# Hybrid decoder trunk on one core: the output projection in two halves of 512 columns, halved constants folded into copies, the first loads in one queue, and a new table of ranks

## The chip, the cores and the metric

The kernel runs on 1 core of one Trainium2 chip. The metric is the device time of one execution in microseconds (us); lower is better. An engine is called here by its short name: PE (TensorE; PEld is its weight load), DVE (VectorE), ACT (ScalarE), POOL (GpSimd), SP (SyncE, which issues most DMAs).

## The reference, cut to what matters

Two layers over x of 512 tokens by 1024 channels, float32. In each layer one input projection feeds four mixers A to D of 256 channels each; their gated outputs are joined and go through one output projection, which is added to the residual. A final RMSNorm ends the trunk.

```python
h = rmsnorm(x, norm_w)
p = split_cols(h @ w_in)            # 1024 x 3380 per layer
o_a = dsa_mixer(...)                # indexer, top 128 of the keys, attention
o_b = nsa_mixer(...)                # compressed, selected and window attention
y = conv3(p['c_c'] * p['c_x'], conv_w);  o_c = p['c_b'] * y
o_d = einsum(causal_pool_mean(d_u) - d_u, pool_w) * pool_scale
mixed = concat([silu(gate_m) * o_m for m in 'abcd'])
x = x + mixed @ w_out               # 1024 x 1024 per layer
```

## The kernel before, in words

**Tiling.** Tokens stand in four tiles of 128 (index `i`), channels in eight blocks of 128 (index `k`). Every product with a large weight is done as three matmuls of split float32 values: high part times high part, high times low, low times high. `lin_tok` (line 603) makes a tile of tokens by `n` columns with 8 x 3 matmuls of `n` columns each into one PSUM bank (tag "mm", two banks); `lin_ch` (line 616) makes 128 channels by 512 tokens.

**Weights.** `load_w` (line 568) brings a group of up to 384 columns in four parts of two channel blocks. A part is: a DMA into a staging tile `st` (four places), a copy to the high part `wh` (ACT; for the very first group, `start=True`, DVE), and a subtraction for the low part `wl` (POOL, one for each channel block; for the first group the second one is DVE's). `wh` and `wl` have six places each of 2 x 384 columns. Two groups of layer 0 stage in the places of `mT` instead (`ws`).

**The start.** `load_x` brings the x tiles by SP's queue, the first weight part goes by ACT's queue (two DMAs, line 582), the other three by SP's. `norm_tile` (line 746) squares each half of an x tile (first half on ACT with a POOL step behind it, second half on DVE: `mean_sq`, line 719), takes the power on POOL, scales on DVE (`xn`), transposes on PE and splits into `hT` (ACT and DVE). 40 transposes of `warm` (line 655) fill PE where nothing else is ready.

**Constants.** `late_constants` (line 703) fills the masks on POOL, issues 14 small DMAs on SP (`cw`, `pw`, `psc`) and then makes two halved copies with POOL: `cwh = 0.5 * cw` and `psh = 0.5 * psc`, which `conv` and `conv_gate_pool` (lines 1196, 1214) read on DVE much later.

**The output projection** of layer `l` (from line 1300): three groups of columns, 256 + 384 + 384 in layer 0 and 384 + 384 + 256 in layer 1; in each group the four token tiles (`out_tile`, line 1309) run over the channel blocks in the order `KORD` = 4, 5, 6, 7 (mixers C, D), 0, 1 (A), 2, 3 (B). DVE adds the residual, ACT squares for the next norm, POOL sums. In layer 0 the next layer's first weight group is loaded and its norm runs beside the last group; in layer 1 `store` (line 1323) scales and writes the result.

**What sets the order.** The whole kernel is recorded (`Tape.record`) as operations in numbered stages (every call of a function marked `staged`). `schedule` (line 396) then writes a fixed order for each engine: at each step the operation that can start soonest by a table of modelled costs (`cost`, line 318), and among those that start within 1 ns the one of the lowest rank; `RANK` (line 195) holds one rank for each stage. An engine runs its list strictly in that order and waits on semaphores. DMAs on SP are in the list too: one that needs no place that is still held is issued as soon as SP is free.

Of the kernel before, what the change touches and what calls it, by code (L numbers as in the profile page):

```python
# [18 lines left out]
P = 128  # L19
# [147 lines left out]
class Weights:  # L167


    def __init__(self, part):  # L170
        self.part, self.parts = part, {}

    def __getitem__(self, h):
        if h not in self.parts:
            self.parts[h] = self.part(h)
        return self.parts[h]
# [7 lines left out]
class Engine:  # L184
# [43 lines left out]
class Tape:  # L228
# [89 lines left out]
    def cost(self, op):  # L318
# [9 lines left out]
        if op.name == "dma_start":  # L328
# [4 lines left out]
            if op.eng == "ACT" and sum(o.eng == "ACT" for o in self.ops) == 2:  # L333
                op.occ += 1280
# [61 lines left out]
    def schedule(self):  # L396
# [49 lines left out]
        while len(order) < len(ops):  # L446
# [23 lines left out]
            if op.name == "dma_start":  # L470
                landing = max(s + 2000, landing) + op.seen - 2000
                op.seen = landing - s
# [914 lines left out]
```

## Time and profile before

| what | us |
|---|---|
| median of 3 runs | 540.31 (540.21 to 543.2) |
| the profiled execution's own time | 540.52 |
| its span, first to last instruction | 538.8 |
| PE busy | 523.2 (97%) |
| DVE, ACT, POOL busy | 410.4, 301.5, 318.0 |

Rows of the profile name an operation as out<-in by the program's tile names; in the timeline the columns are start, time from the first start to the last end of a merged run of like operations, engine, operation, shapes, count, and in brackets the idle time of the engine before it with what ended it. Almost every instruction carries line 523, the one call that plays the list, so tiles tell the rows apart. PE's matmuls overlap: the length of one is more than the distance from one to the next. The granted clock is a share of full speed: 1.00 is 2.4 GHz, 0.5 is 1.2 GHz.

### The profile page before, as it was taken

The numbers are of one execution on the slowest core, as the hardware profiler recorded it, in microseconds if no ns is written. First come the engines' busy times: TensorE is split into PE (matmuls) and PEld (weight loads), VectorE is DVE, ScalarE is ACT, GpSimd is POOL, SyncE is SP. The second block draws the span as 40 slices with busy tenths as digits, with TensorE's granted clock in tenths as the row PEclk, the third lists the DMA queues.
The fourth block names the chain that finished last, engine by engine and source line by source line (L and its number), as shares of the span: only waits on it lengthen the run. The fifth ranks groups of instructions, "written<-read, shape, count | busy, mean of one in ns | idle before, by whom it ended". The sixth has DMA issues, their size and how long they took to land.

```text
span 538.8 us, 9722 instructions
## 1 busy us (share of the span) xinstructions
PE 523.2 (97%) x3091; PEld 459.5 (85%) x3091; DVE 410.4 (76%) x1151; ACT 301.5 (56%) x735; POOL 318.0 (59%) x492
## 2 busy tenths in 40 slices
PE   7979999999999999999999999999999999999995
PEld 6979987778888887899999989778888878789995
DVE  4936799999988868751384689999999987887424
ACT  3447655555648576653245775644366846765422
POOL 5737654475368584836674765447564558693632
PEclk9989999999999999999999999999999999999998
DMA  8960221544133111236751433236413220212204
GB/s 256 260 168 10 77 71 39 128 117 120 31 87 82 37 53 46 54 101 183 207 156 50 119 90 81 49 102 162 110 40 78 61 58 31 88 47 73 78 1 157
DMA packets 74163, 50.63 MB, mean 94 GB/s; under 512 B 23288, under 2 KB 68480, under 8 KB 74112
## 3 DMA queue, kind: packets, MB, share of 16 engines
q1 hardware_dynamic: 73408, 49.38, 33.8%
q10 hardware_dynamic: 704, 0.64, 0.4%
q8 instruction: 24, 0.39, 0.3%
q14 instruction: 27, 0.22, 0.1%
HBM read 45.81 MB, written 4.19 MB: 93 GB/s over the span
## 4 chain that ended last, share of the span: by engine, by line
PE 78%; DVE 11%; DMA 4%; issue 3%; POOL 1%; ACT 1%; SPq 0%; ACTq 0%; POOLq 0%; DVEq 0%
PE mm L523 57%; PE tr L523 10%; PE s L523 6%; PE pv L523 6%; DVE acc L523 5%; DMA st<-in_w_in_dram 3%; DVE m L523 2%; POOL wl L523 1%; DVE qb L523 1%; DMA x<-in_x_dram 1%; DVE qiT L523 1%; SPq L523 0%; ACT qiT L523 0%; ACT wh L523 0%; DMA cw<-in_conv_w_dram 0%
## 5 line engine op out<-in xcount | busy, mean ns | idle before, releaser
L523 POOL TENSOR_TENSOR wl<-st,wh 128x384 fp32r<-128x384 f32 (+4 forms) x188 | 177.9, 974 | 79.2 <-ACT wh L523 63.2
L523 PE MATMUL mm<-hT,wh 128*128 128x512 f32 x544 | 180.4, 403 | 0.7 <-DVE vA L523 0.4
L523 PEld LDWEIGHTS mm<-hT,wh 128*128 128x128 f32 x544 | 99.4, 188 | 19.6 <-DVE vA L523 1.3
L523 PE MATMUL mm<-wh,hT 128*128 128x360 f32 (+3 forms) x480 | 108.6, 310 | 0.5 <-ACT junk L523 0.5
L523 PE MATMUL mm<-hT,wl 128*128 128x512 f32 x272 | 106.5, 400 | 0.0
L523 PE MATMUL mm<-wh,mT 128*128 128x384 f32 (+1 forms) x384 | 90.2, 321 | 0.4 <-DVE x L523 0.4
L523 ACT ACTIVATE wh<-st 128x768 fp32r<-128x768 f32 (+4 forms) x92 | 70.8, 777 | 30.2 <-PE mm L523 17.8
L523 PEld LDWEIGHTS mm<-wh,hT 128*128 128x128 f32 x480 | 80.9, 192 | 1.4 <-ACT junk L523 0.8
L523 PE MATMUL mm<-wl,hT 128*128 128x360 f32 (+3 forms) x240 | 73.2, 311 | 3.1 <-POOL wl L523 3.1
L523 PEld LDWEIGHTS mm<-wh,mT 128*128 128x128 f32 x384 | 66.2, 189 | 2.3 <-DVE x L523 1.0
L523 ACT ACTIVATE pb<-pb,mn 128x128 f32<-128x128 f32 (+3 forms) x96 | 53.3, 557 | 17.9 <-DVE mn L523 17.4
L523 PE MATMUL mm<-wl,mT 128*128 128x384 f32 (+1 forms) x192 | 59.6, 322 | 0.0
L523 PEld LDWEIGHTS mm<-hT,wl 128*128 128x128 f32 x272 | 51.1, 188 | 9.5 <-POOL wl L523 0.8
L523 ACT ACTIVATE ph<-tr 128x512 fp32r<-128x512 f32 x68 | 38.1, 595 | 29.0 <-PE tr L523 22.4
L523 DVE MAX8 m<-acc 128x8 f32<-128x512 f32 (+2 forms) x96 | 51.4, 550 | 0.5
L523 DVE MATCH_REPLACE8 acc<-m,acc 128x512 f32<-128x512 f32 (+2 forms) x96 | 51.7, 541 | 0.0
L523 PEld LDWEIGHTS mm<-wl,hT 128*128 128x128 f32 x240 | 45.8, 192 | 3.9 <-POOL wl L523 3.5
L523 DVE TENSOR_TENSOR pl<-tr,ph 128x512 fp32r<-128x512 f32 x60 | 39.9, 685 | 9.4 <-ACT ph L523 8.4
L523 POOL TENSOR_SCALAR pb<-pb,rs,gt 128x512 f32<-128x512 f32 (+2 forms) x48 | 33.7, 715 | 20.7 <-DVE rs L523 6.6
L523 PE MATMUL tr<-ident,pb 128*128 128x128 f32 x240 | 44.2, 274 | 0.0
L523 DVE TENSOR_TENSOR x<-mm,x 128x256 f32<-128x256 f32 (+2 forms) x32 | 12.7, 420 | 38.3 <-PE mm L523 38.3
L523 PEld LDWEIGHTS tr<-ident,pb 128*128 128x128 f32 x240 | 30.9, 140 | 9.6 <-POOL pb L523 2.1
(162 smaller groups left out, 900.3 us busy)
## 6 DMA issues: line engine op xcount, KB each, us to landing
st<-in_w_in_dram SPq DMA_DIRECT2D x104, 128.0 KB, 2.6
st<-in_w_in_dram SPq DMA_DIRECT2D x28, 256.0 KB, 3.2
st<-in_w_out_dram SPq DMA_DIRECT2D x16, 384.0 KB, 3.4
x<-in_x_dram SPq DMA_DIRECT2D x16, 256.0 KB, 4.2
st<-in_w_in_dram SPq DMA_DIRECT2D x7, 320.0 KB, 3.9
st<-in_w_out_dram SPq DMA_DIRECT2D x8, 256.0 KB, 2.7
x1d<-x SPq DMA_DIRECT2D x8, 256.0 KB, 3.3
x<-x1d SPq DMA_DIRECT2D x8, 256.0 KB, 2.8
```

What stands on the lines that cost most here:

```text
L523: getattr(self.engines[op.eng].real, op.name)(*[real(a) for a in op.args], **{k: real(v) for k, v in op.kw.items()})
```

## The change

- **Output projection.** Two halves of 512 columns (`load_half`, one channel block per part) in both layers; only the last token tile's last half in layer 1 is done as two products of 256 columns. A part is now one DMA of 128 x 512, one ACT copy and one POOL subtraction. The split weights get single places: for half 0 six channel blocks in the places of `wh` and `wl` and two (2, 3) in places of the tag `cd` (tiles of `conv` and `conv_gate_pool`); for half 1 blocks 4 and 5 in those of `sga` and `sgb` (gates of mixers A and B), 6 in `kTA0`, `kTA1`, 7 in `vA`, `kiT`, and 0 to 3 in `wh`, `wl`.
- **Constants.** `cwh` and `psh` are gone: the factor 0.5 stands as `scale=0.5` in two ACT copies that were there already. The 14 DMAs and the clearing of `pw` move to a stage of their own, `channel_constants`, recorded after `compressed`; its rank is 105 (`late_constants`, which had 127, has 72).
- **First loads.** All on SP's queue. The ranks of the first stages put them in the order x tile 0, weight part 0, part 1, x tile 1, part 2, x tile 2, part 3, x tile 3 (11, 17, 20, 21, 22, 23, 24, 25); before it was x tiles 0, 1, 2, then parts 1, 2, then x tile 3, part 3. The copies to `wh` of the first group go from DVE to ACT.
- **First norms.** `early`: for token tile 0 as before; for tiles 1 to 3 both halves are squared on ACT, with a POOL step behind each.
- **Stores.** In layer 1 the second half of every token tile is stored by ACT's queue (before: of the last tile alone).
- **Ranks and cost table.** A new `RANK`, 540 instead of 480 ns for a DMA's issue and longer landings early in the kernel, in the model that orders the work.

```diff
@@ -167,13 +167,15 @@
-    def __init__(self, part):
-        self.part, self.parts = part, {}
-
-    def __getitem__(self, h):
+    def __init__(self, part, per):
+        self.part, self.per, self.parts = part, per, {}
+    def __getitem__(self, k):
+        h = k // self.per
         if h not in self.parts:
             self.parts[h] = self.part(h)
-        return self.parts[h]
+        return self.parts[h][k % self.per]
@@ -193,34 +195,33 @@
 RANK = [
-    1, 0, 577, 3, 5, 0, 576, 28, 38, 2, 6, 4, 29, 34, 27, 42, 0, 30, 39, 22, 40, 0, 45, 43, 44, 12, 0, 32, 0,
...
+    1, 11, 571, 54, 2, 0, 0, 17, 20, 21, 22, 23, 24, 25, 6, 18, 0, 29, 26, 32, 42, 0, 33, 37, 36, 38, 0, 8, 0,
...
 ]
@@ -328,9 +329,9 @@
             rows = n * (out.shape[0] if out is not None else P) * 4 // run
-            op.dur = op.occ = 480
+            op.dur = op.occ = 540
             op.seen = 2000 + rows * (0.56 + run / 437.0)
-            if op.eng == "ACT" and sum(o.eng == "ACT" for o in self.ops) == 2:
+            if op.eng == "ACT" and not any(o.eng == "ACT" for o in self.ops):
                 op.occ += 1280
@@ -468,7 +469,8 @@
             if op.name == "dma_start":
-                landing = max(s + 2000, landing) + op.seen - 2000
+                landing = max(s + 2000, landing)
+                landing += (op.seen - 2000) * (1.4 if landing < 8000 else 1.15 if landing < 15000 else 1.0)
                 op.seen = landing - s
@@ -579,7 +581,7 @@
             for c0, c in segs:
-                (S if start and h == 0 else SP).dma_start(
+                SP.dma_start(
                     st[:, :, o : o + c],
@@ -587,15 +589,26 @@
             wl = wp.tile([P, 2, 384], F32R, name=nm("wl"), tag="wl", bufs=6)
-            if start:
-                V.tensor_copy(wh[:, :, :n], st[:, :, :n])
-            else:
-                S.activation(wh[:, :, :n], st[:, :, :n], AF.Copy)
+            S.activation(wh[:, :, :n], st[:, :, :n], AF.Copy)
             for k in range(2):
                 lo(V if start and k else G, wl[:, k, :n], st[:, k, :n], wh[:, k, :n])
-            return wh, wl
-
-        return Weights(part)
+            return [(wh[:, k, :], wl[:, k, :]) for k in range(2)]
+        return Weights(part, 2)
+    def load_half(src, b, homes):
+        @tape.staged
+        def part(k):
+            st = wp.tile([P, T], F32, name=nm("st"), tag="st", bufs=4)
+            SP.dma_start(st, src[k * P : (k + 1) * P, half(b)])
+            hi, lw = homes(k)
+            S.activation(hi, st, AF.Copy)
+            lo(G, lw, st, hi)
+            return [(hi, lw)]
+        return Weights(part, 1)
@@ -605,8 +618,7 @@
         for k in order:
-            wh, wl = w[k // 2]
-            rh, rl = wh[:, k % 2, c0 : c0 + n], wl[:, k % 2, c0 : c0 + n]
+            rh, rl = (v[:, c0 : c0 + n] for v in w[k])
             st, sp = k == order[0], k == order[-1]
@@ -617,8 +629,7 @@
         for k in range(KC):
-            wh, wl = w[k // 2]
-            lh, ll = wh[:, k % 2, c0 : c0 + P], wl[:, k % 2, c0 : c0 + P]
+            lh, ll = (v[:, c0 : c0 + P] for v in w[k])
             PE.matmul(ps, lh, act[0][:, k, :], start=k == 0, stop=False)
@@ -680,8 +691,6 @@
     pw = const.tile([P, DEPTH, 2, P], F32, name="pw")
-    cwh = const.tile([P, DEPTH, 3, 2], F32, name="cwh")
-    psh = const.tile([P, DEPTH, 2], F32, name="psh")
@@ -706,6 +715,9 @@
                             channel_multiplier=1)
+    @tape.staged
+    def channel_constants():
         G.memset(pw, 0.0)
@@ -713,8 +725,6 @@
             SP.dma_start(psc[:, l, :], pool_scale[l].rearrange("(j p) -> p j", p=P))
-        G.tensor_scalar(cwh, cw, 0.5, 0.0, op0=OP.mult, op1=OP.add)
-        G.tensor_scalar(psh, psc, 0.5, 0.0, op0=OP.mult, op1=OP.add)
@@ -731,11 +741,11 @@
-    def rms(xt, g, ms=None):
+    def rms(xt, g, ms=None, early=False):
             for b in range(2):
-                ms = mean_sq(xt[b], ms, b == 1)
+                ms = mean_sq(xt[b], ms, b == 1 and early)
         G.tensor_tensor(ms, ms, mhalf, OP.pow)
@@ -743,8 +753,8 @@
     @tape.staged
-    def norm_tile(i, xt, g, hT, ms=None):
-        xn = rms(xt, g, ms)
+    def norm_tile(i, xt, g, hT, ms=None, early=False):
+        xn = rms(xt, g, ms, early)
         ts = slice(i * P, (i + 1) * P)
@@ -1196,16 +1206,16 @@
             b = cd()
-            S.activation(b, pb, AF.Copy)
+            S.activation(b, pb, AF.Copy, scale=0.5)
             p = lin_ch(hT, w, P)
             y = cd()
-            V.tensor_scalar(y, u, cwh[:, l, 2, j : j + 1], None, op0=OP.mult)
+            V.tensor_scalar(y, u, cw[:, l, 2, j : j + 1], None, op0=OP.mult)
             for s in (1, 2):
-                V.scalar_tensor_tensor(y[:, s:], u[:, : T - s], cwh[:, l, 2 - s, j : j + 1], y[:, s:], op0=OP.mult,
+                V.scalar_tensor_tensor(y[:, s:], u[:, : T - s], cw[:, l, 2 - s, j : j + 1], y[:, s:], op0=OP.mult,
                                        op1=OP.add)
@@ -1220,7 +1230,7 @@
             u, a, b = cd(), cd(), cd()
-            S.activation(u, ps, AF.Copy)
+            S.activation(u, ps, AF.Copy, scale=0.5)
@@ -1243,7 +1253,7 @@
             PE.matmul(pm, pw[:, l, j, :], a, start=True, stop=True)
-            V.scalar_tensor_tensor(u, pm, psh[:, l, j : j + 1], b, op0=OP.mult, op1=OP.mult)
+            V.scalar_tensor_tensor(u, pm, psc[:, l, j : j + 1], b, op0=OP.mult, op1=OP.mult)
             mixed(6 + j, u)
@@ -1275,6 +1285,8 @@
         compressed(cmp_in)
+        if l == 0:
+            channel_constants()
         w = load_w(win, [(B_GATE, 256)])
@@ -1301,23 +1313,21 @@
         g = load_g(SP, norm_w[l + 1 : l + 2, :] if l + 1 < DEPTH else final_norm_w[None, :])
-        c0 = 0
         ms = [None] * NT
         y = [norm_out() if fin else None for _ in range(NT)]
-        @tape.staged
-        def out_tile(i, w, c0, n):
-            ps = bank("mm", 2)
-            lin_tok(ps, mT, i, w, 0, n, KORD)
-            for b in range(2):
-                a, e = max(c0, b * T), min(c0 + n, (b + 1) * T)
-                if a < e:
-                    r = slice(a - b * T, e - b * T)
-                    xo = xn[i][b][:, r]
-                    V.tensor_add(xo, ps[:, a - c0 : e - c0], xo)
-                    ms[i] = mean_sq(xo, ms[i], e == DM)
-                    if fin:
-                        V.tensor_mul(y[i][b][:, r], xo, g[b][:, r])
+        @tape.staged
+        def out_tile(i, w, b):
+            n = T // 2 if fin and b and i == NT - 1 else T
+            for c in range(0, T, n):
+                ps = bank("mm", 2)
+                lin_tok(ps, mT, i, w, c, n, KORD)
+                xo = xn[i][b][:, c : c + n]
+                V.tensor_add(xo, ps[:, :n], xo)
+                ms[i] = mean_sq(xo, ms[i], b == 1 and c + n == T)
+                if fin:
+                    V.tensor_mul(y[i][b][:, c : c + n], xo, g[b][:, c : c + n])
@@ -1329,21 +1339,40 @@
             S.activation(y[i][1], y[i][1], AF.Copy, scale=ms[i])
-            (S if i == NT - 1 else SP).dma_start(out[i * P : (i + 1) * P, half(1)], y[i][1])
-
-        for n in (384, 384, 256) if fin else (256, 384, 384):
-            w = load_w(w_out[l], [(c0, n)])
-            last = c0 + n == DM
-            if last and not fin:
+            S.dma_start(out[i * P : (i + 1) * P, half(1)], y[i][1])
+        def home(pool, tag, bufs=1):
+            return pool.tile([P, T], F32R, name=nm("w"), tag=tag, bufs=bufs)
+        def homes_0(k):
+            if k in KORD[6:]:
+                return home(wk, "cd", 4), home(wk, "cd", 4)
+            return home(wp, "wh", 6), home(wp, "wl", 6)
+        spare = {}
+        def homes_1(k):
+            j = KORD.index(k)
+            if j < 2:
+                if not spare:
+                    spare.update((s, res.tile([P, 2, T], F32R, name=nm("w"), tag=s)) for s in ("sga", "sgb"))
+                return spare["sga"][:, j, :], spare["sgb"][:, j, :]
+            if j < 4:
+                return [home(res, t) for t in (("kTA0", "kTA1"), ("vA", "kiT"))[j - 2]]
+            return home(wp, "wh", 6), home(wp, "wl", 6)
+        for b, homes in enumerate((homes_0, homes_1)):
+            w = load_half(w_out[l], b, homes)
+            if b and not fin:
                 w_next = first_group(l + 1)
             for i in range(NT):
-                out_tile(i, w, c0, n)
-                if last:
+                out_tile(i, w, b)
+                if b:
                     store(i)
                         norm_tile(i - 1, xn[i - 1], g, hT_next, ms[i - 1])
-            c0 += n
         if not fin:
@@ -1351,7 +1380,7 @@
     def first_norm(i):
-        norm_tile(i, xt0[i], g_first, hT0)
+        norm_tile(i, xt0[i], g_first, hT0, early=i == 0)
```

## Rows read from the trace of the kernel before

**Rows 1.** Page: busy time and share by engine; granted PE clock in 40 slices.

```profile
PE 523.2 (97%) x3091; PEld 459.5 (85%) x3091; DVE 410.4 (76%) x1151; ACT 301.5 (56%) x735; POOL 318.0 (59%) x492
...
PEclk9989999999999999999999999999999999999998
```

**Rows 2.** Stretches: length; busy PE, PEld, DVE, ACT, POOL (instructions); clock, DMA share, GB/s.

```profile
12.00:16.40 4.40, 3.54 (x24) 2.82 (x22) 4.40 (x10) 1.78 (x5) 2.38 (x5) 1.00 1.01 324
20.00:33.00 13.00, 13.00 (x90) 12.85 (x88) 8.60 (x28) 7.76 (x25) 5.55 (x12) 1.00 0.78 163
34.20:37.40 3.20, 0.11 (x1) 0.00 (x0) 0.60 (x2) 0.57 (x2) 1.10 (x4) 1.00 0.55 151
37.40:41.00 3.60, 3.56 (x16) 3.46 (x16) 0.00 (x0) 0.00 (x0) 3.60 (x8) 0.53 0.80 241
```

**Rows 3.** Waits of PE, whole span: total us, times, longest.

```profile
PE mm L523 <- POOL wl L523: 3.1, 1, 3.1
```

**Rows 4.** Timeline, 29 to 38 us: the constants' stage and the weights behind it.

```profile
29.20 1.15 ACT L523 ACTIVATE wh<-ws 128x512 fp32r<-128x512 f32 x2
...
34.62 0.20 POOL L523 TENSOR_SCALAR cwh<-cw 128x12 f32<-128x12 f32 x1 [7.92 <-DMA cw<-in_conv_w_dram]
...
36.50 0.20 POOL L523 TENSOR_SCALAR psh<-psc 128x4 f32<-128x4 f32 x1 [1.68 <-DMA psc<-in_pool_scale_dram]
36.66 2.79 POOL L523 TENSOR_TENSOR wl<-ws,wh 128x256 fp32r<-128x256 f32 x4
...
37.44 0.49 PE L523 MATMUL mm<-wl,hT 128*128 128x256 f32 x1 [3.13 <-POOL wl L523]
```

**Rows 5.** Timeline, 0 to 12 us: first loads, first norm, first matmul.

```profile
0.79 2.91 SPq L523 DMA_DIRECT2D x<-in_x_dram  x6
...
1.42 0.92 ACTq L523 DMA_DIRECT2D st<-in_w_in_dram  x2
...
3.75 4.96 SPq L523 DMA_DIRECT2D st<-in_w_in_dram  x4
...
6.09 0.56 POOL L523 TENSOR_TENSOR ss<-ss,mhalf 128x1 f32<-128x1 f32 x1 [0.88 <-DVE ss L523]
...
8.37 0.54 DVE L523 CAST wh<-st 128x720 fp32r<-128x720 f32 x1 [2.36 <-DMA st<-in_w_in_dram]
...
9.39 1.40 DVE L523 SCALAR_TENSOR_TENSOR xn<-x,ss,s 128x512 f32<-128x512 f32 x2
...
11.80 0.41 PE L523 MATMUL mm<-wh,hT 128*128 128x360 f32 x1
```

**Rows 6.** Groups by shape, PE, in 144:153, 246:255 and 526:532 us: busy us, mean ns.

```profile
L523 PE MATMUL mm<-hT,wh 128*128 128x512 f32 x27 | 8.2, 389 | 0.0
L523 PE MATMUL mm<-hT,wl 128*128 128x512 f32 x14 | 5.3, 389 | 0.0
...
L523 PE MATMUL mm<-wh,mT 128*128 128x384 f32 x35 | 8.8, 334 | 0.0
L523 PE MATMUL mm<-wl,mT 128*128 128x384 f32 x19 | 5.9, 334 | 0.0
...
L523 PE MATMUL mm<-wh,mT 128*128 128x256 f32 x36 | 6.5, 283 | 0.0
L523 PE MATMUL mm<-wl,mT 128*128 128x256 f32 x17 | 4.8, 283 | 0.0
```

**Rows 7.** Groups by shape, POOL, whole span: busy us, mean ns, idle before, releasers.

```profile
L523 POOL TENSOR_TENSOR wl<-st,wh 128x384 fp32r<-128x384 f32 x112 | 115.0, 1054 | 59.6 <-ACT wh L523 46.8 <-PE mm L523 8.9 <-DMA st<-in_w_in_dram 3.4
...
L523 POOL TENSOR_TENSOR wl<-st,wh 128x256 fp32r<-128x256 f32 x40 | 29.6, 768 | 11.1 <-ACT wh L523 10.9
```

**Rows 8.** Chain that ended last, from 499 us: start us, us, what.

```profile
499.07 30.93 PE mm L523 x199
```

**Rows 9.** Timeline, 500 to 503 us, layer 1: the last use of mixer A's gate.

```profile
500.62 0.43 DVE L523 SCALAR_TENSOR_TENSOR om<-om,sg 128x256 f32<-128x256 f32 x1
...
501.31 2.17 POOL L523 TENSOR_TENSOR wl<-st,wh 128x384 fp32r<-128x384 f32 x2 [6.97 <-ACT wh L523]
```

53 rows, old and new, of the table RANK are left out of this document.

## Prediction

> **What bounds the kernel now.** I read the page first. PE is busy 97% of the span and no other engine more than 76% [rows 1]: PE's list of work is the bound nearly everywhere, and time is won by shortening it or by closing the few places where PE stands still or runs slow. The line of granted clock shows where: an 8 in the third slice (27 to 40 us) and one at the end [rows 1]. The waits of PE name one large one, 3.1 us for POOL's low parts of weights [rows 3]. The timeline around it tells why: PE waits until 37.44 us for `wl`; POOL could have made it from about 30 us, since ACT had the high parts ready at 29.20 + 1.15 = 30.35, but POOL stood 7.92 us at `cwh`, for the DMA of the convolution's constants, and 1.68 us more at `psh` [rows 4]. Nobody needs these constants yet. Behind the pause PE is granted 0.53 of its clock from 37.4 to 41 us, that is mostly 1.2 instead of 2.4 GHz [rows 2]. The stretches ahead show the start: between 12 and 16.4 us DVE is busy all of the 4.40 us, the DMA engines are full (324 GB/s), PE has 3.54 of 4.40, part of it filler; from 20 to 33 us PE is full [rows 2].
>
> The sum is made against the profiled execution's own 540.5 us (span 538.8 and 1.7 around it), which is 0.2 above the median of 540.31. About 1% (5.4 us) is what a measurement of this kernel can tell from no change.
>
> **Constants (likely -4.8 us).** The two POOL operations go, and with them both waits. POOL's next four `wl` took 2.79 us [rows 4]; begun at 30.4 they end near 33.2, before PE asks for the first of them at about 34.3 (37.44 - 3.13). So the 3.13 us of standing go. The clock: 37.4 to 41 us holds 16 matmuls of 256 columns in 3.56 us [rows 2]; at the full-clock distance found below (0.118 us) they take 1.9, so 1.7 us more go with the pause, if the low clock follows from it, as its place right behind it says. 3.1 + 1.7 = 4.8. Bounds: 2.4, if half of it comes back as a wait for the next thing POOL is late with, and 4.8; a loss is excluded, because an operation and its wait leave POOL's list and DVE reads the constants only in `conv`. The 14 small DMAs stay on SP's queue. Their rank puts them later, but having nothing to wait for they will still go out in the first gaps, ahead of weights for later groups as now; cost nothing, since PE is full from 20 to 33 us with them in the queue [rows 2]. If that cover goes, it is a late weight part and belongs to rival 1.
>
> **Start (likely -2.5 us).** The power for x tile 0 is ready at 6.09 + 0.56 = 6.65 us, but DVE scales the tile only at 9.39: in its list the first CAST stands ahead, waiting 2.36 us for weight part 0 until 8.37, then a `wl` [rows 5]. The first matmul starts at 11.80. Part 0 is that late because ACT's two issues at 1.42 share the DMA engines with six x loads of SP [rows 5]; in the new order it is second in line, and the cast is ACT's. So DVE can scale 9.39 - 6.65 = 2.7 us earlier, and the transposes and the first matmul follow. DVE, full from 12 to 16.4 us [rows 2], also loses four casts and three squaring passes; ACT, which takes them, is busy 1.78 of those 4.40 us and has room. What follows is fed in the order in which it is used. Upper bound 2.7 + (4.40 - 3.54) = 3.6 us, if PE also becomes full in that stretch; lower bound -0.9 (a loss), the 0.92 us that ACT's queue spent on issuing and SP's now spends [rows 5], if the rest is paced by DMA throughput. I take 2.5, near the gap that one can read off DVE's list. It carries through to the end, because PE is the bound behind it.
>
> On the issue: the Trainium skill, "DMA: Bandwidth & Descriptors" (section "Issuing engines are not separate DMA queues"), says that DMAs of all issuing engines run on the same 16 DMA engines and that a second issuing engine saves only issue time. That speaks against the change, for it gives up that saving. The trace agrees in part: SP's six x issues take 2.91 us, the next four 4.96 us with the DMA engines full [rows 5]: they wait for throughput, not for issue. By the rule alone the term would be 2.5 - 0.9 = 1.6; I leave it at 2.5.
>
> **Output projection (likely -1.0 us).** The distance of matmuls in full stretches is (stretch + one length) / count of those that touch it [rows 6]: 512 columns (9.0 + 0.389) / 41 = 0.229 us; 384: (9.0 + 0.334) / 54 = 0.173; 256: (6.0 + 0.283) / 53 = 0.1185. A block of 1024 columns costs 2 x 0.173 + 0.1185 = 0.4645 before, 2 x 0.229 = 0.458 after: 6.5 ns less. There are 2 layers x 4 tiles x 24 = 192 of them: 1.25 us. The last tile's split gives back 24 x (0.237 - 0.229) = 0.2. So 1.0. The fixed part of the matmuls saved (192 fewer, 24 more by the split) is the whole gain there. Weights: POOL's `wl` takes 1.054 us at 384 and 0.768 at 256 columns [rows 7], so 1.34 at 512 (estimate on the line through both), 8 x 1.34 = 10.7 a half against 22.0 us of PE work (96 x 0.229): hidden, with little room where the halves meet (rival 2). The tail behind the last matmul keeps its 256 columns and its steps; storing more by ACT's queue costs nothing, since those are early tiles.
>
> On the distance: the Trainium skill, "TensorE: Matmul & The Clock Gate" (section "Back-to-back issue gap"), gives N / 2.4 + 2.5 ns for an isolated matmul at full clock, a smaller fixed part than the rows have. By it a block saves 2.5 ns and the term would be 0.5 us; the rows decide.
>
> **Order of the rest (0, bounds -3 and +3).** All ranks change. PE idles 538.8 - 523.2 = 15.6 us in all [rows 1]; 3.1 is counted, and most of the rest is start and tail. What remains, and the slack hidden in busy time, I bound by 3 us both ways, as an estimate. I take 0.
>
> **Sum.** 540.5 - 4.8 - 2.5 - 1.0 = 532.2 us.
>
> **Rivals.**
> 1. *POOL stays the supplier that is late* (537.1 us). PE comes earlier to the second early group, whose low parts are also POOL's, so half of the constants' gain returns as a shorter pause and the start's gain ends in the same wait: 540.5 - 2.4 - 1.0. For it: PE's only large wait is for `wl` [rows 3]. Against: POOL gets 9.6 us of waiting back [rows 4] and is busy 5.55 of 13 us before [rows 2].
> 2. *The halves meet badly* (541.8 us, slower than before). Blocks 4 and 5 of half 1 take the places of mixer A's gate, last read at 500.62 + 0.43 = 501.05 in layer 1 [rows 9]. 199 of 288 matmuls are still ahead at 499.07 [rows 8], so 89 x 0.173 = 15.4 us of projection are done there; of the 22.0 us of half 0 then 6.6 are left, to 505.7. POOL makes blocks 4, 5 from about 501.7 (one ACT copy) to 504.4 and 0 to 3 to 509.7; PE, after 12 matmuls of half 1, wants block 0 at 508.4 and block 3 at 510.5. That holds with 0.8 us to spare, if 6 and 7 are made before in POOL's idle 6.97 us [rows 9]. If they are not, or the copies stand in ACT's list behind something late, PE pauses. A pause like the one at 34 us cost 4.8 with its low clock; one per layer makes 532.2 + 9.6. It decides once POOL has about 0.8 us more to do. Against: the second PSUM bank gives 2.75 us of other work.
> 3. *The new order also wins in the middle* (529.2 us): the bound of -3. For it: the landings in the model that orders the work come later, so loads are planned earlier. Against: little of PE's idle time lies there.
>
> **Chances.** Forecast 0.52, rival 1 0.20, rival 2 0.14, rival 3 0.14. The forecast's own range is 529.5 to 535. The whole range, 527 to 540, takes in rivals 1 and 3 with their bounds and leaves out most of rival 2. Faster by over 1% (below 534.9): rival 3 and nearly all of the forecast, 0.64. Within 1%: rival 1, most of rival 2 and the forecast's rest, 0.30. Slower by over 1% (above 545.7): rival 2 with the start's gain gone too, 0.06.
>
> **What would show it.** Right: no POOL wait for `cw` or `psc`; PE has no wait near 34 us and full clock from the start to the tail; the first `hT` matmul near 9.3 us; the projection's 512-column matmuls 0.229 us apart without a PE wait for `wl` at the change of halves; PE's idle time down from 15.6 us by 3 or more. Wrong: a second slice of low clock, a PE wait for `wl` between 30 and 60 us (rival 1) or in the projection (rival 2), a first matmul at 11 us or later.

## The result, and the profile after

The kernel after takes 538.66 us (median of 20 executions, 531.98 to 540.23) beside 541.29 for the kernel before (20 executions): ratio 0.9926, 95% interval 0.9905 to 0.9948. By this ratio, which goes by the mean of the executions, the gain is some 4.0 us; the two medians differ by 2.6 us. Forecast were 8.3 us less. The single executions tell more than the median: four of the 20 took 531.98 to 533.68, the other sixteen 536.8 to 540.2. The mean granted clock was 0.998 or 0.999 in each of the four and 0.990 to 0.996 in the sixteen. The profiled one (538.69, span 536.8) belongs to the sixteen.

The page of the profile after: busy times, then the two lines that answer to [rows 1].

```profile
PE 521.5 (97%) x2923; PEld 442.2 (82%) x2923; DVE 418.3 (78%) x1119; ACT 303.6 (57%) x723; POOL 307.6 (57%) x462
...
PE   8999999999999999999999999999969999999995
...
PEclk9999999999999999999999999999979999999998
```

The 8 that the granted clock had in its third slice is gone. A 7 has come where nothing was: slice 30, 389 to 403 us, in layer 1. PE's own line has a 6 in the same slice. The waits of PE, which answer to [rows 3], name the new pause:

```profile
PE tr L525 <- DVE pl L525: 4.5, 1, 4.5
PE tr L525 <- POOL ident L525: 1.7, 1, 1.7
PE mm L525 <- ACT w L525: 1.1, 1, 1.1
```

The 3.1 us for POOL's `wl` are gone, 4.5 us for DVE's `pl` are there. The windows, the first four over the stretches of [rows 2], the last two around the new pause (columns: us, then busy and count of PE, PEld, DVE, ACT, POOL; granted clock, DMA share, GB/s):

```profile
12.00:16.40 4.40, 4.24 (x31) 3.79 (x29) 3.29 (x6) 3.64 (x9) 3.66 (x7) 1.00 1.07 361
20.00:33.00 13.00, 13.00 (x92) 12.79 (x91) 7.29 (x26) 7.57 (x23) 7.75 (x17) 1.00 0.47 92
34.20:37.40 3.20, 3.20 (x29) 3.20 (x28) 2.57 (x9) 1.66 (x7) 2.97 (x7) 1.00 0.91 319
37.40:41.00 3.60, 3.60 (x33) 3.60 (x32) 2.40 (x10) 3.16 (x8) 0.87 (x2) 1.00 0.43 158
393.90:398.80 4.90, 0.44 (x3) 0.05 (x3) 4.90 (x4) 0.00 (x0) 3.33 (x4) 0.75 0.55 147
396.40:403.20 6.80, 4.43 (x15) 3.77 (x16) 5.65 (x16) 2.42 (x9) 0.83 (x1) 0.50 0.47 115
```

The pause at 34 to 37 us and the low clock behind it have gone as forecast: PE is full there at 1.00. The last two rows show the same pair again, only later and larger: PE stands for most of 4.9 us, and from 396.4 to 403.2 us it is granted 0.50, that is 1.2 instead of 2.4 GHz. The timeline from 389 to 400 us tells what DVE was doing:

```profile
391.41 5.82 POOL L525 TENSOR_TENSOR wl<-st,wh 128x384 fp32r<-128x384 f32 x6
...
391.61 5.91 DVE L525 TENSOR_SCALAR cd<-cd,cw 128x512 f32<-128x512 f32 x1
...
393.91 0.40 PE L525 MATMUL pv<-ph,vB 128*128 128x512 f32 x1
...
397.44 0.68 DVE L525 MAX8 m<-acc 128x8 f32<-128x512 f32 x1
398.04 1.26 DVE L525 TENSOR_TENSOR pl<-tr,ph 128x512 fp32r<-128x512 f32 x2
...
398.77 0.48 PE L525 MATMUL tr<-ident,pb 128*128 128x128 f32 x1 [4.46 <-DVE pl L525]
```

One DVE operation, the convolution's first product `cd = cd * cw`, takes 5.91 us. It begins 0.20 us after the start of the first of six `wl` subtractions that POOL runs back to back, and ends 0.29 us after the end of the sixth. Behind it in DVE's list stand a `MAX8` and the `pl` for which PE waits. The operations of the tile `cw`, after and then before, show how unusual that is (durations min/median/max in ns, then first and last start):

```profile
L525 DVE TENSOR_SCALAR cd<-cd,cw x4: 476/960/5910, 138.3 to 430.8; 128x512 f32<-128x512 f32 x4
```

```profile
L523 DVE TENSOR_SCALAR cd<-cd,cwh x4: 582/757/1306, 148.4 to 430.9; 128x512 f32<-128x512 f32 x4
```

The chain of work that ended last, followed back between 375 and 410 us, runs through it:

```profile
391.69 5.83 DVE cd L525
397.52 0.60 DVE m L525
398.12 0.60 DVE pl L525
398.77 0.48 PE tr L525
```

To see where the time went over the whole span, take for each trace the time from the span's start less what PE's matmuls begun by then would take at the distances of [rows 6] (about 8.5 ns each, plus 0.434 ns a column; the 40 transposes of `warm` count as nothing). What is left is the time that PE has lost so far, idle, slow or on filler. It is an estimate, worked out from the start of every other matmul in the trace:

| lost in us between | before | after | difference |
|---|---|---|---|
| start and 33 us | 14.0 | 11.9 | -2.1 |
| 33 and 60 (constants) | 7.1 | 2.2 | -5.0 |
| 60 and 240 (layer 0) | 12.8 | 11.1 | -1.7 |
| 240 and 300 (projection of layer 0, change of layers) | 3.0 | 5.2 | +2.2 |
| 300 and 385 | 6.3 | 5.5 | -0.8 |
| 385 and 410 (the new pause) | 2.1 | 8.6 | +6.5 |
| 410 and the end | 12.3 | 12.7 | +0.4 |
| work of all matmuls | 481.2 | 479.7 | -1.4 |

Up to rounding the sum is -2.0, the difference of the two spans (538.8 and 536.8). By 385 us the kernel after has lost 7.4 us less than the one before; 6.5 of them are given back at one place. A second trace of the kernel after (e0_again below) differs from this one by up to 0.8 us in a row, so smaller differences mean nothing.

### The profile page after: what moved, and what is told of

It is laid out like the page before. It is cut to its first block, busy times and chain, and to the rows that moved or that the text cites. A ratio compares the mean times of both kernels' runs of the same rounds, so it can differ in the third digit from the quotient of the medians.

```text
span 536.8 us, 9306 instructions
## 1 busy us (share of the span) xinstructions
PE 521.5 (97%) x2923; PEld 442.2 (82%) x2923; DVE 418.3 (78%) x1119; ACT 303.6 (57%) x723; POOL 307.6 (57%) x462
## 4 chain that ended last, share of the span: by engine, by line
PE 77%; DVE 7%; DMA 5%; POOL 4%; issue 3%; ACT 2%; SPq 1%; POOLq 0%; ACTq 0%; DVEq 0%
PE mm L525 56%; PE tr L525 9%; PE s L525 7%; PE pv L525 4%; DMA st<-in_w_in_dram 2%; POOL wl L525 2%; DMA x<-in_x_dram 2%; DVE cd L525 2%; DMA st<-in_w_out_dram 1%; POOL pb L525 1%; SPq L525 1%; DVE pl L525 1%; ACT wh L525 1%; DVE acc L525 1%; POOL w L525 1%
## 5 line engine op out<-in xcount | busy, mean ns | idle before, releaser
L525 POOL TENSOR_TENSOR wl<-st,wh 128x384 fp32r<-128x384 f32 (+4 forms) x140 | 131.4, 962 | 76.5 <-ACT wh L525 66.4
L525 PE MATMUL mm<-wh,hT 128*128 128x360 f32 (+3 forms) x480 | 107.0, 308 | 0.0
L525 PE MATMUL mm<-w,mT 128*128 128x512 f32 (+1 forms) x408 | 99.0, 384 | 1.1 <-ACT w L525 1.1
L525 PEld LDWEIGHTS mm<-w,mT 128*128 128x128 f32 x408 | 71.9, 188 | 16.3 <-ACT w L525 2.8
L525 ACT ACTIVATE wh<-st 128x768 fp32r<-128x768 f32 (+4 forms) x72 | 55.5, 781 | 29.7 <-DMA st<-in_w_in_dram 17.7
L525 ACT ACTIVATE pb<-pb,mn 128x256 f32<-128x256 f32 (+3 forms) x96 | 53.4, 558 | 29.0 <-DVE mn L525 28.6
L525 DVE MATCH_REPLACE8 acc<-m,acc 128x384 f32<-128x384 f32 (+2 forms) x96 | 51.8, 543 | 0.0
L525 DVE MAX8 m<-acc 128x8 f32<-128x384 f32 (+2 forms) x96 | 51.2, 551 | 0.4
L525 POOL TENSOR_TENSOR w<-st,w 128x512 fp32r<-128x512 f32 x32 | 41.9, 1322 | 12.9 <-ACT w L525 11.2
L525 DVE CUSTOM_DVE_ANT_0 pb<-s,mask 128x128 f32<-128x128 f32 (+3 forms) x72 | 32.7, 462 | 10.3 <-PE s L525 3.6
```

Source lines behind the costliest of these rows:

```text
L525: getattr(self.engines[op.eng].real, op.name)(*[real(a) for a in op.args], **{k: real(v) for k, v in op.kw.items()})
```

## Experiments

**The theory (A).** The new order puts the convolution's product of layer 1 beside an unbroken run of POOL subtractions. DVE and POOL exclude each other there, and the product gets in only when the run breaks. PE's pause and its low clock follow. The rivals put the loss in something else: in the product's operands or its place in DVE's list, whatever POOL does, or in other parts of the new order, so that the pause only stands where the time would be lost anyway. In the experiments on the pause, every engine's list keeps the order that the kernel after has; either the convolution's four first products go to another engine, or one POOL operation is added.

**The kernel after once more (e0_again).**

> The changed kernel as it is. Theory A (one DVE product of the convolution in layer 1 is kept out by POOL's run of six low parts, in most executions and not in all): times fall in groups, one near 532 to 534 us without the pause of PE and one near 538 to 540 with it; in a profile with the pause the product lasts 5 to 6 us, in one without it under 1.3 us. Theory B (the product is long for a reason of its own, such as late input): the same times, and the length does not follow POOL's run. Theory C (the gains of the start and of the constants are smaller than forecast and there is no group below 535): all times 537 to 540.

Measured: 539.13 us (10 executions, 532.24 to 539.87), ratio 0.994 (0.9911 to 0.9968). Again one execution was quick (532.24) and nine took 537.7 to 539.9. The product and the run, in this trace's timeline:

```profile
391.57 5.80 POOL L525 TENSOR_TENSOR wl<-st,wh 128x384 fp32r<-128x384 f32 x6
391.78 5.87 DVE L525 TENSOR_SCALAR cd<-cd,cw 128x512 f32<-128x512 f32 x1
```

So the long product is no accident of one profile. The half clock lasted only 3.4 us here, all of it while PE worked, and between 385 and 410 us 8.4 us were lost, close to the 8.6 above.

**The four products on ACT (e1_conv_act).** If it is DVE that POOL keeps out, the product runs on ACT beside POOL's run without waiting.

```diff
-V.tensor_scalar(y, u, cw[:, l, 2, j : j + 1], None, op0=OP.mult)
+S.activation(y, u, AF.Copy, scale=cw[:, l, 2, j : j + 1])
```

> The four first products of the convolution (two per layer) done by ACT instead of DVE, all else in the same order. Theory A: the pause of PE near 394 us is gone in every execution, full clock from the start to the tail, times 531 to 534 us, ratio to the kernel before 0.982 to 0.987, with a spread of about 1 us. Theory B (late input): ACT's product waits as long, PE pauses 4 to 5 us, 537 to 540 us as before the edit. Theory C: 537 to 540 us.

Measured: 533.08 us (5 executions, 532.47 to 535.14), ratio 0.9858 (0.9837 to 0.9879). POOL's run is as long as ever, and no product is held up:

```profile
391.80 0.73 ACT L527 ACTIVATE cd<-cd,cw 128x512 f32<-128x512 f32 x1
392.13 5.89 POOL L529 TENSOR_TENSOR wl<-st,wh 128x384 fp32r<-128x384 f32 x6
```

PE has no wait for `pl`, and the granted clock is a 9 in every slice. This takes the product away from DVE, which also shortens DVE's list; the next two leave it there.

**One break in POOL's run, behind the first subtraction (e2_pause_1) or the third (e2_pause_3).** POOL copies one column of the product's result, so it must wait until the product is done. That adds work to POOL and takes none from DVE.

```diff
 lo(G, wl...)          # first (third) of the six in layer 1
+G.tensor_copy(probe, y[:, 0:1])
 lo(G, wl...)
```

> The product stays on DVE in the same place; after the first of the six low parts POOL copies one column of the product's result, so that it waits until the product is done. Theory A: the product lasts at most 1.5 us (the rest of one low part and its own 0.5), no pause of PE near 394 us, 531 to 534 us. Theory B: the product lasts 5 to 6 us as before, POOL waits for it, and the time is 538 us or more.

> The same with POOL's wait behind the third of the six low parts. Theory A: in executions where the product is kept out, it lasts about 3 low parts less what passed before it came, 2.8 + 0.5 = 3.3 us, and PE pauses about 2 us instead of 4.6; times between those of the two other kernels, 533 to 536 us. Theory B: the length does not change with the place of the wait.

Measured: with the break behind the first 531.97 us (531.15 to 533.25), ratio 0.9833 (0.9812 to 0.9855); behind the third 534.07 (533.46 to 534.8), ratio 0.9871 (0.9853 to 0.9888); four executions each. The timelines, first with the early break, then with the late one:

```profile
390.82 1.00 POOL L531 TENSOR_TENSOR wl<-st,wh 128x384 fp32r<-128x384 f32 x1
391.03 1.08 DVE L531 TENSOR_SCALAR cd<-cd,cw 128x512 f32<-128x512 f32 x1
...
392.17 0.18 POOL L530 COPY probe<-cd 128x1 f32<-128x1 f32 x1 [0.35 <-DVE cd L531]
392.31 4.92 POOL L531 TENSOR_TENSOR wl<-st,wh 128x384 fp32r<-128x384 f32 x5
```

```profile
392.00 2.96 POOL L531 TENSOR_TENSOR wl<-st,wh 128x384 fp32r<-128x384 f32 x3
392.21 3.03 DVE L531 TENSOR_SCALAR cd<-cd,cw 128x512 f32<-128x512 f32 x1
...
395.30 0.18 POOL L530 COPY probe<-cd 128x1 f32<-128x1 f32 x1 [0.35 <-DVE cd L531]
```

The product lasts as long as the run that it met: 1.08 us behind one subtraction, 3.03 behind three, 5.87 behind six. The time follows: 531.97, 534.07, 539.13. An added POOL operation with a wait makes the kernel 7.2 us faster, 539.13 - 531.97. That shows theory A for this place, and it shows that the pause isn't a loss that would come anyway. That a product gets in only at a break is no rule for every run of POOL: the last section shows cases where it got in without one. PE's wait for `pl` was 4.4 us with six, 1.6 with three, and isn't among the waits with one; with three, the granted clock stayed at 1.00 behind it.

**The constants alone (e3_before_const).** The kernel before in its own order, without the two halved copies.

```diff
-G.tensor_scalar(cwh, cw, 0.5, 0.0, op0=OP.mult, op1=OP.add)
-G.tensor_scalar(psh, psc, 0.5, 0.0, op0=OP.mult, op1=OP.add)
...
-S.activation(b, pb, AF.Copy)
+S.activation(b, pb, AF.Copy, scale=0.5)
...
-S.activation(u, ps, AF.Copy)
+S.activation(u, ps, AF.Copy, scale=0.5)
```

> The kernel before, in its own order, without the two halved copies of the constants on POOL (the factor 0.5 stands in two ACT copies), nothing else changed. Theory (constants, 4.8 us): POOL has no wait for the constants' DMA, PE has no pause near 34 us, the clock is full from 7 us to the tail; 536.7 us where the kernel before has 541.5, ratio 0.989 to 0.993. Rival (half of it returns as a wait for the next low parts): 539 us, ratio 0.995 to 0.997, and PE waits 1 to 2 us for wl between 34 and 50 us.

Measured: 535.51 us (6 executions, 534.76 to 536.08) beside 541.51, ratio 0.989 (0.9869 to 0.991): 6.0 us. In the timeline POOL now makes the low parts where it stood 7.92 us before [rows 4]:

```profile
29.72 2.83 POOL L526 TENSOR_TENSOR wl<-ws,wh 128x256 fp32r<-128x256 f32 x4 [3.17 <-ACT wh L526]
```

They end at 32.55 (the forecast said 33.2), PE waits for no `wl`, and the granted clock is full up to the tail.

**DVE's list at the start alone (e4_before_start).** The kernel before, with the split of weight part 0 moved behind the scaling of x tile 0.

```diff
 order of the first operations
-cast part 0 (DVE), wl (DVE), wl (POOL), scale x tile 0 (DVE, two)
+scale x tile 0 (DVE, two), cast part 0 (DVE), wl (DVE), wl (POOL)
```

> The kernel before with one change of order: the first three operations that split weight part 0 (the cast and the low part on DVE, the low part on POOL) stand behind the scaling of x tile 0 instead of ahead of it. Theory (the start's 2.5 us come from DVE's list): DVE scales at about 6.7 us instead of 9.4, the first hT matmul starts near 9.5 us instead of 11.8, and the time falls by about 2.5 us to 539.0, ratio 0.994 to 0.997. Rival (the first weights and x tiles arrive no earlier, so PE only waits later): the first matmul is earlier by up to 1 or 2 us, but the last of the first 96 matmuls still starts near 32.8 us and the time stays within 0.5 us of 541.5.

Measured: 541.54 us (12 executions, 540.6 to 542.03), ratio 1.0001 (0.9988 to 1.0013): nothing. The edit did what it was to do, in the timeline:

```profile
6.68 1.41 DVE L529 SCALAR_TENSOR_TENSOR xn<-x,ss,s 128x512 f32<-128x512 f32 x2 [0.68 <-POOL ss L529]
...
8.37 0.54 DVE L529 CAST wh<-st 128x720 fp32r<-128x720 f32 x1 [0.28 <-DMA st<-in_w_in_dram]
...
10.34 0.41 PE L529 MATMUL mm<-wh,hT 128*128 128x360 f32 x1
...
12.37 0.60 PE L529 MATMUL mm<-wh,hT 128*128 128x360 f32 x2 [0.91 <-DVE hT L529]
```

The first scaling comes 2.71 us sooner (6.68 for 9.39) and the first matmul 1.46 us sooner (10.34 for 11.80), but PE then waits for what comes next, and by 33 us it has lost 13.9 us, and 14.0 in the kernel before.

The remaining runs stand on the version with the early break, whose pause is gone, so that smaller terms can be seen.

**That version again (e2_pause_1b), the projection in products of 256 (e5_proj_256), part 0 by ACT's queue (e6_act_queue), the first copies on DVE (e7_dve_cast).**

```diff
 e5: each of the 360 products of 512 columns
-matmul(ps, lhs, w[:, 0:512])
+matmul(ps[:, 0:256], lhs, w[:, 0:256]); matmul(ps[:, 256:512], lhs, w[:, 256:512])
 e6: part 0
-SP.dma_start(st, ...)
+S.dma_start(st, ...)
 e7: the first four parts
-S.activation(wh, st, AF.Copy)
+V.tensor_copy(wh, st)
```

> The version with POOL's wait behind the first low part once more, as the base of the next three: 531 to 533 us, ratio to the kernel before 0.981 to 0.986.

> On that base, each of the 360 output projection matmuls of 512 columns is issued as two of 256. Theory (a fixed part of 8 ns per matmul, 2 x 0.1185 - 0.229): 360 x 0.008 = 2.9 us more than the base, about 535. Rival (no fixed part, the width does not matter): within 0.5 us of the base.

> On that base, the two DMAs of the first weight part go by ACT's queue, as in the kernel before. Theory of the prediction (the first loads are paced by the DMA engines' throughput, not by issue): within 0.5 us of the base, the first hT matmul near 9.0 us. The rule that a second issuing engine saves issue time: up to 0.9 us less than the base. A rival on the other side (part 0 in parallel with x tile 0 delays x tile 0): first matmul later by about 1 us and 0.5 to 1 us more than the base.

> On that base, the four first casts to the high part are done by DVE again instead of ACT, in the same places of the order. Theory (DVE's load in the first 20 us costs PE time): up to 2.1 us of DVE work more; the first matmul at 9.0 to 9.5 us and 0.5 to 2 us more than the base. Rival (only the order in DVE's list mattered, not who casts): within 0.5 us of the base.

Measured, beside 541.52 for the kernel before, measured together:

| version | us, median (lowest to highest) | ratio (interval) |
|---|---|---|
| e2_pause_1b | 533.55 (532.41 to 534.31) | 0.9854 (0.9835 to 0.9872) |
| e5_proj_256 | 536.09 (535.11 to 537.84) | 0.9907 (0.9888 to 0.9926) |
| e6_act_queue | 532.56 (532.23 to 535.09) | 0.9847 (0.9827 to 0.9867) |
| e7_dve_cast | 531.29 (531.11 to 532.63) | 0.9819 (0.9801 to 0.9837) |

360 more matmuls over the same columns cost 536.09 - 533.55 = 2.5 us, about 7 ns each (the two intervals leave some 4 to 12): the fixed part that the term of the projection rests on. ACT's queue for part 0 makes no difference outside the intervals. The first copies on DVE are not slower; whether they are faster stays open, since the base itself moved by 1.6 us between two measurements (531.97 and 533.55, the second above the 531 to 533 expected).

**The copies on DVE again (e7_dve_cast_b), and with it the loads in the order and the queues of before (e8_old_loads).**

```diff
 e8, order of the first loads (base of both: e7)
-SP: x0, part 0, part 1, x1, part 2, x2, part 3, x3
+SP: x0, x1, x2, part 1, part 2, x3, part 3;  ACT: part 0
```

> The version with POOL's wait and the first casts on DVE once more, as the base of the next one and to see whether its 531.3 us hold: 531 to 532.5 us, ratio 0.980 to 0.985; by 33 us of the span PE is 2.5 us of work ahead of the kernel before.

> On that base, the loads of x and of the first weight group go out in the order and by the queues of the kernel before (x tiles 0, 1, 2 on SP with weight part 0 on ACT's queue, then parts 1, 2, x tile 3, part 3). Theory (the start's gain is the order of the loads, which brings part 0 and 1 before x tiles 1 and 2): first hT matmul at 10.5 us or later, PE 2 to 3 us of work less by 33 us, 2 to 3 us more than the base. Rival (the gain is in the engines' lists and the order of the loads does not matter): within 0.5 us of the base.

Measured: 531.41 us (5 executions, 530.97 to 531.73), ratio 0.9803 (0.978 to 0.9825), and 533.77 (533.13 to 534.22), ratio 0.9848 (0.9828 to 0.9869). The old order and queues cost 2.4 us; since part 0 on ACT's queue made no difference in e6, that is put down to the order. With the old one the first cast waits longer for its part:

```profile
0.79 2.81 SPq L542 DMA_DIRECT2D x<-in_x_dram  x6
...
7.94 0.54 DVE L537 CAST wh<-st 128x720 fp32r<-128x720 f32 x1 [0.86 <-DMA st<-in_w_in_dram]
...
10.15 0.41 PE L542 MATMUL mm<-wh,hT 128*128 128x360 f32 x1
```

With the new one that cast starts at 6.99 and the first matmul at 9.65. Only 0.9 us of the loss stands by 33 us (12.6 us lost against 11.7; 2 to 3 were expected there), the rest builds up to 150 us (22.4 against 19.8); through which waits wasn't followed. The version with the copies on DVE has the lowest times of all: 1.8% and 2.0% below the kernel before in its two measurements, where the kernel after is 0.7% below.

## Why the prediction was right and wrong

The likeliest case, 532.2 us, is near what the kernel takes when the new pause isn't there: the two versions that take the pause away need 531.97 to 533.55 in three measurements. Four of 20 executions (531.98 to 533.68) are as quick; their clock of 0.998 or more says that at least the low clock was missing, the rest is inferred. In most executions the pause is there, and 538.66 is what was measured. That the sum comes out so well without the pause is in part luck, because the terms below err both ways. The range (527 to 540) holds it. The gain was within 1%, which had a chance of 0.30.

**The step that failed: "Order of the rest (0, bounds -3 and +3)".** It bounded the new order by PE's idle time of before, which is the right bound for what an order can win. It is none for what an order can lose: a new order can make a wait that the old one didn't have, and the clock that falls behind it isn't in the idle time either. The new pause cost 6.5 us in the profile, about the sum of two parts: 4.46 of standing, and 2.2 as half of the 4.4 us that PE then worked at half clock (it was halved for 6.8 us, but for 2.4 of them PE still stood). The prediction had read the same pair at 34 us and priced it at 4.8, and in rival 2 it priced "a pause like the one at 34 us" at another place. What was missing was a rival for a DVE operation held up by POOL. Rows could have pointed to it: all ranks change, DVE has work in three quarters of the span and POOL in 59%, and in the trace of before the product's time already ran from 582 to 1306 ns in the same shape.

**How the order came about.** The code has the exclusion: `cost` marks such DVE operations with `locks`, and `schedule` starts each at the end of the POOL operation that holds the pair, then POOL behind it. So in the model the product waits for one subtraction at most. On the chip POOL's next one began with no gap in between, five times over. In the trace of before the chip did as the model says, with the same product (last section). A break of 0.35 us between two of them was enough to let it in.

**Constants (-4.8).** Right in cause and mechanism, and under-sized: alone it measured -6.0. Rival 1 (POOL stays late) fell: PE waits for no `wl` in either trace.

**Start (-2.5).** Right in size (2.1 us by 33 us in the profile, 2.7 and 2.8 in the two traces of the version with the early break), wrong in its mechanism: the gap "that one can read off DVE's list" is real, and closing it alone brought nothing. Of the parts tried, the order of the loads has a price, 2.4 us in all. The copies' move to ACT has none or a small cost. That part 0's issue moved to SP's queue, the lower bound of -0.9, didn't show either.

**Projection (-1.0).** The distance of matmuls was right: at the measured 7 ns each, the 168 matmuls that the kernel after has fewer are worth 1.2 us, where 1.0 was forecast (the 1.4 in the table is worked out at 8.5 ns, not measured). So was the length of POOL's subtraction at 512 columns, 1.34 by the estimate; the page's costliest groups say 1322 ns:

```profile
L525 POOL TENSOR_TENSOR w<-st,w 128x512 fp32r<-128x512 f32 x32 | 41.9, 1322 | 12.9 <-ACT w L525 11.2 <-ACT pb L525 0.9 <-POOL cd L525 0.2
```

The gain was eaten all the same. Rival 2 (the halves meet badly) came about in small, in layer 0, and not through POOL: the copies were late, and not behind other work in ACT's list, as it has it, but for their DMA. The timeline where the second half begins has

```profile
247.84 0.63 ACT L525 ACTIVATE w<-st 128x512 fp32r<-128x512 f32 x1 [2.22 <-DMA st<-in_w_out_dram]
248.52 7.83 PE L525 MATMUL mm<-w,mT 128*128 128x512 f32 x33 [1.09 <-ACT w L525]
```

ACT waits 2.22 us for the weights' DMA and PE 1.09 for ACT. From 240 to 300 us 2.2 us more are lost than before; the versions without the pause lose 4.2 to 5.4 us there, beside 3.0. No run undid this part, so how much of the 2.2 belongs to the halves and how much to the change of layers stays open.

**Rival 3** (the new order wins in the middle): between 60 and 240 us the kernel after lost 1.7 us less than before in one trace and 0.8 less in the other, the version with the early break 0.2 less and 0.9 more; nothing that can be told from no change.

**What was to show it** worked as far as it went: no wait for constants, full clock at 34 us, first matmul at 9.46 us (said: near 9.3). PE's idle time fell only from 15.6 to 15.3 us, where 3 or more was said, because the new pause took back what the old one had cost. The sign that it was wrong, "a second slice of low clock", is what led to the place.

Open is why some executions of the same kernel are quick (four of 20, one of 10): no profile of such a one was taken. The last section has an observation that would fit. What the two at 536.8 us did isn't known either.

## What to carry to other kernels

When an order is rewritten, price what it can lose as well as what it can win: look for every DVE operation with its data in SBUF that may come to stand beside a run of POOL operations, and ask what waits behind it. A pause of PE costs more than its length where the granted clock falls behind it, so one slice of low clock on the page is the first thing to look for. Moving such an operation to ACT, or one wait in POOL's run, gave 6 to 7 us here.

## What the runs showed of the hardware that was not expected

A DVE multiplication of 128 x 512 floats by a column of factors, SBUF to SBUF, takes 0.48 us at its shortest. Begun 0.2 us into a run of POOL subtractions of 1.0 us each, it ended 0.3 us behind the run's end: after 1.08, 3.03 and 5.87 us with one, three and six of them. It got in at none of the boundaries in between. POOL wasn't slowed: the six took 5.80 us beside the waiting product and 5.89 without one. In the same kernel the two later steps of the convolution, which also read and write SBUF on DVE but with two large inputs, took at most 1.38 us:

```profile
L525 DVE SCALAR_TENSOR_TENSOR cd<-cd,cw,cd x8: 716/746/1382, 139.0 to 432.3; 128x511 f32<-128x511 f32 x4, 128x510 f32<-128x510 f32 x4
```

It doesn't always lose. In the trace of before, the same product (there `cd<-cd,cwh`) came into a run of seven and got in behind the subtraction that it met; POOL's next one then took 1.20 us instead of 1.0:

```profile
143.08 7.05 POOL L523 TENSOR_TENSOR wl<-st,wh 128x384 fp32r<-128x384 f32 x7 [9.47 <-ACT wh L523]
148.38 0.88 DVE L523 TENSOR_SCALAR cd<-cd,cwh 128x512 f32<-128x512 f32 x1
```

Another DVE multiplication of 128 x 512, SBUF to SBUF, of tile `acc`, did both beside runs of three, first in e2_pause_1, then in e7_dve_cast_b:

```profile
420.30 2.95 POOL L531 TENSOR_TENSOR wl<-st,wh 128x384 fp32r<-128x384 f32 x3
421.46 2.07 DVE L531 TENSOR_SCALAR acc<-acc 128x512 f32<-128x512 f32 x1
```

```profile
420.87 3.17 POOL L534 TENSOR_TENSOR wl<-st,wh 128x384 fp32r<-128x384 f32 x3
422.53 0.65 DVE L534 TENSOR_SCALAR acc<-acc 128x512 f32<-128x512 f32 x1
```

The kept traces have 20 cases in which one of these two multiplications began during a `wl` subtraction of 384 columns with another directly behind it. The eight that began 0.10 to 0.21 us into the subtraction waited for the run's end (or for the break put into it); the twelve that began 0.27 to 0.65 us into it got in behind that subtraction. If the moment of the start decides, a shift of under 0.1 us would free the product of layer 1, which would fit that some executions are quick. No run moved the start alone, so this is an observation and not a shown cause.

The Trainium skill, "SBUF — State Buffer" (section "Who interferes with whom"), says that such a DVE operation can take a pair of ports that it shares with GpSimd, that the one issued first has it for its whole instruction, and that the other is blocked until then. The traces agree: in the long run the product is blocked and POOL is not, and in the trace of before POOL waits once DVE has got in. Read as one instruction's length, the rule would allow a delay of up to 1.0 us; the measured 5.4 (5.87 - 0.48) show that a waiting DVE operation can lose to every POOL instruction of an unbroken run.

The fixed part of a matmul came out as 7 ns from 360 added ones. The Trainium skill, "TensorE: Matmul & The Clock Gate" (section "Back-to-back issue gap"), gives a fixed part of 2.5 ns for an isolated matmul at full clock, by which they would have cost 0.9 us instead of 2.5; the measurement decides.
